# A batched-expert MLP on one core: the first four experts' input in other pieces, and one token order for all experts

## The chip, the cores and the metric

The kernel runs on 1 core of one Trainium2 chip. The metric is the device time of one execution in microseconds (us), as the median of several runs.

## What is computed

Eight experts, each with 256 tokens of 512 values, go through two layers with a ReLU between them:

```python
n_experts, capacity, hidden, expert_hidden = 8, 256, 512, 2048
...
h = np.matmul(x, w1)
h = np.maximum(h, 0)
return np.matmul(h, w2).astype(np.float32)
```

All arrays are float32. x and the output have 4.19 MB each, w1 and w2 33.6 MB each.

## The kernel before, in words

**Data.** The kernel computes in bf16. GpSimd (POOL) issues the weight loads as DMAs that cast float32 to bf16 on the way; both w1 and w2 have buffers for two experts (w1_sb, w2_sb). A load for expert e+2 waits until the first layer of expert e (for w1, semaphore s_first) or its second layer (for w2, s_act) is done. w2 of the last expert comes in two halves (s_w2 and s_w2b). x of experts 4 to 7 is also a casting DMA of POOL, into x_c. x of experts 0 to 3 comes in float32 on SP's queue into x_f, in three transfers (lines 107 to 109): expert 0 with 4 KB per partition, experts 1 and 2 together with 8 KB, expert 3 with 4 KB, each with a semaphore of its own.

**Transposing x.** Four rounds, two experts each. In a round DVE casts the even expert and ACT the odd one into x_b (line 200), PE transposes both through PSUM (L305), and DVE and ACT copy the result into xe (L216 or L225). xe holds x with the hidden index on the partitions and the tokens along the free axis. PE does all four rounds before its first matmul of the layers.

**Token order.** For pairs of experts the outputs are stored with four consecutive rows of the pair per partition, so that one partition's run in DRAM is 8 KB long. The order of the tokens within xe and ht decides which output row ends on which partition. Before the change the copies into xe produce the order that the first three pairs want, with one form for experts 0 and 3 and another for the others (lines 215 to 228); the last pair, stored per expert, has its order changed in the ReLU (lines 243 to 245).

**Layers.** For each of four pairs: first layer of both experts (64 matmuls each, L321, the weights from w1_sb, 256 tokens of xe as moving operand), ReLU by DVE and ACT from PSUM into ht (lines 248, 250), then second layer of both (32 matmuls each, L341) and copies into o_sb (L260). The program of PE is a hardware loop; addresses that change come from registers (function ahead).

**Who lets PE go on.** SP counts tokens for PE: it waits for a weight transfer's semaphore and then increments t_w, which PE takes before a first layer, before a second layer and, for the last expert, before its second half of w2 (kt = 8). SP also waits for s_xe, the copies into xe, ahead of the first experts' tokens.

**The end.** When the second layer of expert 6 is done (s_go), SP stores the first three pairs in one DMA of 3 MB (L137). Then it stores expert 6 in pieces: odd rows (64 partitions), every fourth row from 2 on (32 partitions), a token for PE in between, every fourth row in the middle (16 partitions) and the rest from a copy o_low (L149), and last expert 7 (512 KB) when its copies are done. In the code:

```python
sp.wait_ge(s_w2[e + b], 16).then_inc(t_w, 1)
store(E - 2, slice(1, P, 2))
store(E - 2, slice(2, P, 4))
sp.wait_ge(s_w2b, 16).then_inc(t_w, 1)
...
store(E - 2, slice(L, P - L, 4))
```

Of the kernel before, what the change touches and what calls it, by code (L numbers as in the profile page):

```python
# [9 lines left out]
def kernel(  # L10
# [7 lines left out]
    nc = tc.nc  # L18
# [26 lines left out]
    J = G * MT  # L45
    x_r = x.rearrange("e (p m) k -> p e m k", m=MT)
    x_pair = x[1:3].rearrange("e c k -> (e c) k").rearrange("(p s m) k -> p s m k", p=P, m=MT)
    x_rows = x[G:].rearrange("e c k -> (e c) k").rearrange("(p j) k -> p j k", p=P)


    x_f = nc.alloc_sbuf_tensor("x_f", [P, G, MT, H], f32)
    x_c = nc.alloc_sbuf_tensor("x_c", [P, J, H], bf)
    x_b = nc.alloc_sbuf_tensor("x_b", [P, 2, KT1 * MT, P], bf)
    xe = nc.alloc_sbuf_tensor("xe", [P, E * KT1 * C], bf)
# [18 lines left out]
    s_x = [sem(f"s_x{i}") for i in range(3)]  # L73
# [29 lines left out]
    def load_x(eng, e, n, src, i):  # L103
        ins = eng.dma_start(x_f[:, e:e + n], src).then_inc(s_x[i], 16)
        return ins.ins.name

    tc.no_tile_sem_insts.add(load_x(sp, 0, 1, x_r[:, :1], 0))
    tc.no_tile_sem_insts.add(load_x(sp, 1, 2, x_pair, 1))
    tc.no_tile_sem_insts.add(load_x(sp, G - 1, 1, x_r[:, G - 1:G], 2))
# [12 lines left out]
    for e in range(0, E, 2):  # L122
        for b in range(2):

            if e < G:
                sp.wait_ge(s_xe[b], e // 2 + 1)
                if e + b == 1:
                    sp.wait_ge(s_xe[0], 2)
            elif e + b == G:
                for s in s_xe:  # L130
                    sp.wait_ge(s, G)
            sp.wait_ge(s_w1[e + b if e else 0], 16).then_inc(t_w, 1)
        for b in range(2):
# [8 lines left out]
            else:  # L142
                sp.wait_ge(s_w2[e + b], 16).then_inc(t_w, 1)
                store(E - 2, slice(1, P, 2))
                store(E - 2, slice(2, P, 4))
                sp.wait_ge(s_w2b, 16).then_inc(t_w, 1)
    store(E - 2, slice(L, P - L, 4))
# [21 lines left out]
    pool.dma_start(x_c[:], x_rows).then_inc(s_xc, 16)  # L169
# [25 lines left out]
    def cast(eng, r, b):  # L195

        a = 2 * r + b
        src = x_f[:, a] if a < G else x_c[:, MT * (a - G):MT * (a - G + 1)]
# [6 lines left out]
    def take_x(eng, b):  # L205
        copy = act.copy if eng is act else dve.tensor_copy
        for r in range(G):
            if r < G // 2:
                eng.wait_ge(s_x[(2 * r + b + 1) // 2], 16)
            elif r == G // 2:  # L210
                eng.wait_ge(s_xc, 16)
            cast(eng, r, b)
            eng.wait_ge(s_tr, 2 * r + b + 1)
            a, n = 2 * r + b, KT1 * C
            if a in (0, G - 1):
                copy(  # L216
# [71 lines left out]

    def ahead(flat, weights, first, places, n, step=1):
        by = flat[:].bitcast(mybir.dt.uint8)
        aps = []
        for k in places:
# [87 lines left out]
```

## Time and profile before

| | |
|---|---|
| median of 3 runs | 178.99 us (178.84 to 178.99) |
| profiled execution: time, span | 178.96 us, 177.6 us |
| mean granted TensorE clock | 0.979 of full speed |
| busy: PE, DVE, ACT, POOL | 130.6 (74%), 39.5 (22%), 40.0 (23%), 10.3 (6%) us |
| DMA: POOL's casting queue, SP's queue | 34.60 MB and 91.6%, 6.29 MB and 8.7% of 16 engines' span |
| HBM read, written | 71.30 MB, 4.19 MB |
| chain that ended last | PE L341 2%, ACT L260 0.3% of the span |

The profile shows one execution. The span runs from the first to the last instruction; the time is 1.36 us longer. Bytes of a DMA are counted as they are written, so a cast from float32 to bf16 counts half of what it reads. DMA share is the mean busy share of 16 engines; over short stretches it can pass 1, since a packet counts where it starts.

### The profile page before, as it was taken

What the parts mean: (1) busy time and instruction counts of PE and PEld (TensorE: products, weight loads), DVE (VectorE), ACT (ScalarE), POOL (GpSimd) and SP (SyncE); (2) the same over time, 40 slices, a digit from 0 to 9 for tenths busy, and PEclk for the clock granted to TensorE, in tenths of its full rate; (3) what the DMA queues carried; (4) which work ended last, traced back from release to release, by engine and by line L of the source; (5) the groups of instructions that cost most, each with busy time, mean ns of one, the idle gap of its engine ahead of it and who ended that gap; (6) DMA issues with size and microseconds to landing.
All of it is one profiled execution on the core that took longest, in us unless ns stands there. A gap on an engine that the chain in (4) does not pass through costs nothing. (4 is left out here: it accounts for less than half of the span.)

```text
span 177.6 us, 2364 instructions
## 1 busy us (share of the span) xinstructions
PE 130.6 (74%) x832; PEld 88.9 (50%) x832; DVE 39.5 (22%) x54; ACT 40.0 (23%) x56; POOL 10.3 (6%) x22
## 2 busy tenths in 40 slices
PE   0034430598979699999969595979499695999890
PEld 0024420487854248788424485954134594874340
DVE  0142420123310306333030331320300431230101
ACT  2464520022220203323020222220200321220301
POOL 2400000001010101011010101010100200000000
PEclk9999999999999999999999999999969998799999
DMA  6999999999999999999999999999999999999998
GB/s 232 330 234 207 236 207 207 236 207 207 236 207 207 236 207 207 236 207 207 236 207 207 236 210 203 236 207 207 236 210 203 236 210 203 236 194 212 290 428 352
DMA packets 3720, 40.90 MB, mean 230 GB/s; under 512 B 392, under 2 KB 392, under 8 KB 904
## 3 DMA queue, kind: packets, MB, share of 16 engines
q0 software_dynamic: 2560, 34.60, 91.6%
q1 hardware_dynamic: 1160, 6.29, 8.7%
HBM read 71.30 MB, written 4.19 MB: 425 GB/s over the span
## 5 line engine op out<-in xcount | busy, mean ns | idle before, releaser
L321 PE MATMUL pt_h<-xe,w_sb 128*128 x512 | 65.3, 284 | 17.8 <-PEq L99 17.8
L321 PEld LDWEIGHTS pt_h<-xe,w_sb 128*128 x512 | 57.5, 147 | 26.2 <-issue 24.3
L341 PE MATMUL pt_o<-w_sb,ht_sb 128*128 x256 | 58.3, 386 | 8.7 <-PEq L99 8.7
L341 PEld LDWEIGHTS pt_o<-w_sb,ht_sb 128*128 x256 | 24.8, 99 | 40.9 <-issue 13.7
L250 DVE TENSOR_SCALAR ht_sb<-pt_h 128x512 bf16<-128x512 f32 x32 | 22.1, 692 | 56.1 <-PE pt_h L321 56.1
L248 ACT ACTIVATE ht_sb<-pt_h 128x512 bf16<-128x512 f32 x32 | 19.1, 597 | 61.4 <-PE pt_h L321 61.4
L260 DVE COPY out_sb<-pt_o 64x512 f32 (+1 forms) x14 | 9.6, 689 | 61.9 <-PE pt_o L341 61.8
L260 ACT COPY out_sb<-pt_o 64x512 f32 (+1 forms) x14 | 8.1, 582 | 59.3 <-PE pt_o L341 59.2
L305 PE MATMUL pt_tr<-identity,x_b 128*128 128x128 bf16 x64 | 7.5, 310 | 16.3 <-PEq L99 16.3
L305 PEld LDWEIGHTS pt_tr<-identity,x_b 128*128 128x128 bf16 x64 | 6.5, 144 | 17.0 <-issue 17.0
L159 POOL DMA_DIRECT2D w_sb<-in_w_dram x6 | 3.2, 534 | 74.6 <-ACTq L252 74.6
L225 DVE COPY xe<-pt_tr 128x1024 bf16<-128x1024 bf16 x3 | 3.3, 1088 | 7.9 <-PE pt_tr L305 7.9
L164 POOL DMA_DIRECT2D w_sb<-in_w_dram x5 | 2.6, 528 | 41.2 <-ACT out_sb L260 41.2
L225 ACT COPY xe<-pt_tr 128x1024 bf16<-128x1024 bf16 x3 | 3.6, 1196 | 6.1 <-PE pt_tr L305 6.1
L200 ACT CAST x_b<-x_f 128x1024 bf16<-128x1024 f32 x2 | 4.0, 1988 | 2.2 <-DMA x_f<-in_x_dram 2.2
L200 DVE CAST x_b<-x_f 128x1024 bf16<-128x1024 f32 x2 | 2.1, 1064 | 4.1 <-DMA x_f<-in_x_dram 4.1
L216 DVE COPY xe<-pt_tr 128x1024 bf16<-128x1024 bf16 x1 | 1.2, 1225 | 4.5 <-PE pt_tr L305 4.5
L200 ACT COPY x_b<-x_c 128x1024 bf16<-128x1024 bf16 x2 | 2.2, 1084 | 0.0
L156 POOL DMA_DIRECT2D w_sb<-in_w_dram x2 | 2.0, 1006 | 0.1
L200 ACT ACT_TABLE_LOAD x1 | 1.3, 1283 | 2.9 <-PEq L111 2.9
L216 ACT COPY xe<-pt_tr 128x1024 bf16<-128x1024 bf16 x1 | 1.0, 1012 | 2.0 <-PE pt_tr L305 2.0
L200 DVE COPY x_b<-x_c 128x1024 bf16<-128x1024 bf16 x2 | 1.4, 676 | 0.0
(10 smaller groups left out, 3.7 us busy)
## 6 DMA issues: line engine op xcount, KB each, us to landing
w_sb<-in_w_dram POOLq DMA_DIRECT2D x11, 2048.0 KB, 25.8
w_sb<-in_w_dram POOLq DMA_DIRECT2D x2, 4096.0 KB, 36.7
out_dram<-out_sb SPq DMA_DIRECT2D x1, 3072.0 KB
w_sb<-in_w_dram POOLq DMA_DIRECT2D x2, 1024.0 KB, 25.7
x_f<-in_x_dram SPq DMA_DIRECT2D x2, 512.0 KB, 4.7
x_f<-in_x_dram SPq DMA_DIRECT2D x1, 1024.0 KB, 5.3
x_c<-in_x_dram POOLq DMA_DIRECT2D x1, 1024.0 KB, 9.3
out_dram<-out_sb SPq DMA_DIRECT2D x1, 512.0 KB
```

The costliest lines, as they stand in the source:

```text
L156: pool.dma_start(dst.rearrange("p (e k) n -> p e k n", e=2), src).then_inc(s[0], 16)
L159: pool.dma_start(w1_k[:, e % 2 * KT1:(e % 2 + 1) * KT1], w1_r[e]).then_inc(s_w1[e], 16)
L164: pool.dma_start(w2_k[:, k:k + KT2], w2_r[e]).then_inc(s_w2[e], 16)
L200: copy(x_b[:, b].rearrange("p (t m) q -> p t m q", m=MT), src.rearrange("p m (q t) -> p t m q", t=KT1),).then_inc(t_xb, 1)
L216: copy(xe[:, a * n:(a + 1) * n].rearrange("p (j f r) -> p j f r", f=2, r=R), pt[b][:].rearrange("p j (r f) -> p j f r", f=2),).then_inc(s_ ...
L225: copy(xl[:, :, :, f, :, i].rearrange("p l j q -> p j l q"), pt[b][:].rearrange("p j (l q) -> p j l q", l=l),).then_inc(s_xe[b], 1)
L248: act.activation(dst, src, relu).then_inc(t_h, 1)
L250: dve.tensor_relu(dst, src).then_inc(t_h, 1)
L260: ins = copy(dst, src)
L305: ins = pe.transpose(pt[b][:, j], x_b[:, b, j], identity[:])
L321: ins = pe.matmul(ph[i // 2][:, i % 2, :], ws[i % 2 * KT1 + kt], xs[kt], start=(kt == 0), stop=(kt == KT1 - 1),)
L341: ins = pe.matmul(po[:, m], hs[(kt - k0) * MT + m], ws[kt - k0], start=(kt == 0), stop=(kt == KT2 - 1),)
```

## The change

x of expert 0 comes in two transfers of 2 KB per partition (one row of x each), and x of experts 1 to 3 in one transfer of 12 KB per partition. The first has semaphore s_x0, which now reaches 32, the second s_x1. A partition holds six consecutive rows of the three experts' 768, so that each of the three casts and transposes touches tokens of all three experts, and the copies into xe write every third element (every fourth for experts 4 to 7, which had a step of two). xe is laid out by hidden block and row half, with all 1024 token pairs side by side in natural order, so the moving operand of a first-layer matmul is two runs of 128 columns instead of one of 256. The change of order for the first three pairs is now made in their ReLU, and the last pair's ReLU reads in order. SP waits ahead of expert 1's token for the copies of experts 0 to 3. The store of 32 partitions of expert 6 follows the wait for s_w2b instead of standing ahead of it.

```diff
@@ -42,16 +42,17 @@
-    J = G * MT
-    x_r = x.rearrange("e (p m) k -> p e m k", m=MT)
-    x_pair = x[1:3].rearrange("e c k -> (e c) k").rearrange("(p s m) k -> p s m k", p=P, m=MT)
-    x_rows = x[G:].rearrange("e c k -> (e c) k").rearrange("(p j) k -> p j k", p=P)
-
-
-    x_f = nc.alloc_sbuf_tensor("x_f", [P, G, MT, H], f32)
-    x_c = nc.alloc_sbuf_tensor("x_c", [P, J, H], bf)
+    W = E * P
+    PARTS = ((0, 1), (1, G), (G, E))
+
+    def x_rows(e0, e1):
+        return x[e0:e1].rearrange("e c k -> (e c) k").rearrange("(p j) k -> p j k", p=P)
+
+    x_f = nc.alloc_sbuf_tensor("x_f", [P, MT * G, H], f32)
+    x_c = nc.alloc_sbuf_tensor("x_c", [P, MT * (E - G), H], bf)
     x_b = nc.alloc_sbuf_tensor("x_b", [P, 2, KT1 * MT, P], bf)
-    xe = nc.alloc_sbuf_tensor("xe", [P, E * KT1 * C], bf)
+    xe = nc.alloc_sbuf_tensor("xe", [P, KT1 * MT * W + W - P], bf)
+    xe_j = xe[:, :KT1 * MT * W].rearrange("p (j t) -> p j t", t=W)
     w1_sb = nc.alloc_sbuf_tensor("w1_sb", [P, 2 * KT1 * F + KT2], bf)
     w2_sb = nc.alloc_sbuf_tensor("w2_sb", [P, 2 * KT2 * H], bf)
     ht = nc.alloc_sbuf_tensor("ht_sb", [P, 2 * KT2, H], bf)
@@ -70,7 +71,7 @@
     pt = [nc.alloc_psum_tensor(f"pt_tr{b}", [P, KT1 * MT, P], bf) for b in range(2)]
     sem = nc.alloc_semaphore
-    s_x = [sem(f"s_x{i}") for i in range(3)]
+    s_x = [sem(f"s_x{i}") for i in range(2)]
     s_xc = sem("s_xc")
     s_out = sem("s_out")
     s_go = sem("s_go")
@@ -100,13 +101,11 @@
-    def load_x(eng, e, n, src, i):
-        ins = eng.dma_start(x_f[:, e:e + n], src).then_inc(s_x[i], 16)
-        return ins.ins.name
-
-    tc.no_tile_sem_insts.add(load_x(sp, 0, 1, x_r[:, :1], 0))
-    tc.no_tile_sem_insts.add(load_x(sp, 1, 2, x_pair, 1))
-    tc.no_tile_sem_insts.add(load_x(sp, G - 1, 1, x_r[:, G - 1:G], 2))
+    for s, (e0, e1) in zip(s_x, PARTS):
+        step = 1 if e0 == 0 else MT * (e1 - e0)
+        for j in range(0, MT * (e1 - e0), step):
+            ins = sp.dma_start(x_f[:, MT * e0 + j:MT * e0 + j + step], x_rows(e0, e1)[:, j:j + step])
+            tc.no_tile_sem_insts.add(ins.then_inc(s, 16).ins.name)
     tc.close()
     tc.compile()
@@ -122,13 +121,10 @@
     for e in range(0, E, 2):
         for b in range(2):
-            if e < G:
-                sp.wait_ge(s_xe[b], e // 2 + 1)
-                if e + b == 1:
-                    sp.wait_ge(s_xe[0], 2)
-            elif e + b == G:
-                for s in s_xe:
-                    sp.wait_ge(s, G)
+            for e0, e1 in PARTS:
+                if e + b == e0:
+                    for i in range(2 if e0 else 1):
+                        sp.wait_ge(s_xe[i], (e1 + 1 - i) // 2)
             sp.wait_ge(s_w1[e + b if e else 0], 16).then_inc(t_w, 1)
         for b in range(2):
             if e + b == E - 1:
@@ -142,8 +138,8 @@
             else:
                 sp.wait_ge(s_w2[e + b], 16).then_inc(t_w, 1)
                 store(E - 2, slice(1, P, 2))
-                store(E - 2, slice(2, P, 4))
                 sp.wait_ge(s_w2b, 16).then_inc(t_w, 1)
+    store(E - 2, slice(2, P, 4))
     store(E - 2, slice(L, P - L, 4))
     sp.wait_ge(s_low, 1)
     sp.dma_start(out_q[::4, ::3], o_two).then_inc(s_out, 16)
@@ -166,7 +162,7 @@
             pool.dma_start(w2_k[:, k:k + CUT], w2_r[e, :, :CUT]).then_inc(s_w2[e], 16)
             pool.dma_start(w2_k[:, k + CUT:k + KT2], w2_r[e, :, CUT:]).then_inc(s_w2b, 16)
-    pool.dma_start(x_c[:], x_rows).then_inc(s_xc, 16)
+    pool.dma_start(x_c[:], x_rows(G, E)).then_inc(s_xc, 16)
     load_pair(w1_k, w1, s_w1)
     pool.memset(identity[:], 0.0).then_inc(s_id, 1)
     pool.wait_ge(s_id, 1)
@@ -195,7 +191,7 @@
     def cast(eng, r, b):
         a = 2 * r + b
-        src = x_f[:, a] if a < G else x_c[:, MT * (a - G):MT * (a - G + 1)]
+        src = x_f[:, MT * a:MT * (a + 1)] if a < G else x_c[:, MT * (a - G):MT * (a - G + 1)]
         copy = act.copy if eng is act else dve.tensor_copy
         copy(
             x_b[:, b].rearrange("p (t m) q -> p t m q", m=MT),
@@ -205,27 +201,17 @@
     def take_x(eng, b):
         copy = act.copy if eng is act else dve.tensor_copy
         for r in range(G):
-            if r < G // 2:
-                eng.wait_ge(s_x[(2 * r + b + 1) // 2], 16)
-            elif r == G // 2:
-                eng.wait_ge(s_xc, 16)
+            a = 2 * r + b
+            for s, (e0, e1) in zip((*s_x, s_xc), PARTS):
+                if e0 <= a < min(e0 + 2, e1):
+                    eng.wait_ge(s, 16 if a else 16 * MT)
             cast(eng, r, b)
             eng.wait_ge(s_tr, 2 * r + b + 1)
-            a, n = 2 * r + b, KT1 * C
-            if a in (0, G - 1):
-                copy(
-                    xe[:, a * n:(a + 1) * n].rearrange("p (j f r) -> p j f r", f=2, r=R),
-                    pt[b][:].rearrange("p j (r f) -> p j f r", f=2),
-                ).then_inc(s_xe[b], 1)
-            else:
-                e0, l = (1, 2) if a < G else (G, G)
-                f, i = (a - e0) % 2, (a - e0) // 2
-                xl = xe[:, e0 * n:(e0 + l) * n].rearrange(
-                    "p (l j f q i) -> p l j f q i", l=l, j=KT1 * MT, f=2, i=l // 2)
-                copy(
-                    xl[:, :, :, f, :, i].rearrange("p l j q -> p j l q"),
-                    pt[b][:].rearrange("p j (l q) -> p j l q", l=l),
-                ).then_inc(s_xe[b], 1)
+            e0, e1 = next(part for part in PARTS if part[0] <= a < part[1])
+            copy(
+                xe_j[:, :, e0 * P:e1 * P].rearrange("p j (q i) -> p j q i", i=e1 - e0)[:, :, :, a - e0],
+                pt[b][:],
+            ).then_inc(s_xe[b], 1)
@@ -240,9 +226,9 @@
                     k = KT2 * b + FB * q + FB // 2 * half
                     dst, i = ht[:, k:k + FB // 2, :C], NQ * b + q + 1
                     src = ph[half][:]
-                    if last:
-                        dst = dst.rearrange("p k (m r f) -> p k m r f", m=MT, f=2)
-                        src = src.rearrange("p k (m f r) -> p k m r f", m=MT, f=2)
+                    if not last:
+                        dst = dst.rearrange("p k (m f r) -> p k m f r", m=MT, f=2)
+                        src = src.rearrange("p k (m r f) -> p k m f r", m=MT, f=2)
                     eng.wait_ge(s_h, i)
                     if eng is act:
                         act.activation(dst, src, relu).then_inc(t_h, 1)
@@ -288,11 +274,13 @@
-    def ahead(flat, weights, first, places, n, step=1):
+    def ahead(flat, weights, first, places, n, step=1, rows=1):
         by = flat[:].bitcast(mybir.dt.uint8)
         aps = []
         for k in places:
             ap = by[:, bass.ds(first + 2 * k, 2 * n * step)].bitcast(bf)
+            if rows > 1:
+                ap = ap.rearrange("p (m n) -> p m n", m=rows)[:, :, :P]
             aps.append(ap if step == 1 else ap.rearrange("p (n s) -> p n s", s=step)[:, :, 0])
             pe.lower_ap(aps[-1], for_matmul_weights=weights)
         return aps
@@ -307,7 +295,7 @@
     with pe.Fori(0, G) as g:
         with pe.Fori(0, 2) as b:
-            xs = ahead(xe, False, g * (4 * KT1 * C) + b * (2 * KT1 * C), [kt * C for kt in range(KT1)], C)
+            xs = ahead(xe, False, g * (4 * P) + b * (2 * P), [kt * MT * W for kt in range(KT1)], MT * W, rows=MT)
             take(t_w)
             with pe.Fori(0, NQ) as q:
                 for i in range(FB):
```

The instructions of SP, before. These are its DMAs in program order, with the semaphores waited for ahead of each; x_f is x in float32, out_sb the output on chip:

```order
L104 DMA x_f<-in_x_dram 128x1024
L104 DMA x_f<-in_x_dram 128x2048
L104 DMA x_f<-in_x_dram 128x1024
...
L137 DMA out_dram<-out_sb 128x3x2048 [waits barrier_Pool_Activation_PE_DVE_SP_release,s_w1_0,s_xe0,s_xe1,s_w2_0,s_dve,s_act,s_w1_2,s_w1_3,s_w2_2,s_w2_3,s_w1_4,s_w1_5,s_w2_4,s_w2_5,s_w1_6,s_w1_7,s_w2_6,s_go]
L120 DMA out_dram<-out_sb 64x1024 [waits s_dve,s_w2_7,s_act]
L120 DMA out_dram<-out_sb 32x1024
L120 DMA out_dram<-out_sb 16x1024 [waits s_w2b]
L149 DMA out_dram<-out_sb 8x2x1024 [waits s_low]
L120 DMA out_dram<-out_sb 128x1024 [waits s_dve,s_act]
```

And of the changed kernel:

```order
L107 DMA x_f<-in_x_dram 128x512 x2
L107 DMA x_f<-in_x_dram 128x3072
...
L133 DMA out_dram<-out_sb 128x3x2048 [waits barrier_Pool_Activation_PE_DVE_SP_release,s_w1_0,s_xe0,s_xe1,s_w2_0,s_dve,s_act,s_w1_2,s_w1_3,s_w2_2,s_w2_3,s_w1_4,s_w1_5,s_w2_4,s_w2_5,s_w1_6,s_w1_7,s_w2_6,s_go]
L119 DMA out_dram<-out_sb 64x1024 [waits s_dve,s_w2_7,s_act]
L119 DMA out_dram<-out_sb 32x1024 [waits s_w2b]
L119 DMA out_dram<-out_sb 16x1024
L145 DMA out_dram<-out_sb 8x2x1024 [waits s_low]
L119 DMA out_dram<-out_sb 128x1024 [waits s_dve,s_act]
```

The x transfers are 2 + 1 instead of 1 + 1 + 1, and the wait for s_w2b has moved ahead of the store of 32 partitions.

ACT's part in the four rounds before (x_b is the cast input of the transposes, pt_tr their output):

```order
L200 CAST x_b<-x_f 128x1024 [waits s_x1]
L225 COPY xe<-pt_tr 128x8x2x64 [waits s_tr]
L200 CAST x_b<-x_f 128x1024 [waits s_x2]
L216 COPY xe<-pt_tr 128x1024 [waits s_tr]
L200 COPY x_b<-x_c 128x1024 [waits s_xc]
L225 COPY xe<-pt_tr 128x8x4x32 [waits s_tr]
```

And in the changed kernel:

```order
L196 CAST x_b<-x_f 128x1024 [waits s_x1]
L211 COPY xe<-pt_tr 128x8x128 [waits s_tr]
L196 CAST x_b<-x_f 128x1024
L211 COPY xe<-pt_tr 128x8x128 [waits s_tr]
L196 COPY x_b<-x_c 128x1024 [waits s_xc]
L211 COPY xe<-pt_tr 128x8x128 [waits s_tr]
```

The casts are as many as before; s_x1 now stands for experts 1 to 3, and all copies into xe have one form.

## Rows read from the trace of the kernel before

**Rows 1.** The page's 40 slices of the span: busy tenths of the DMA engines.

```profile
DMA  6999999999999999999999999999999999999998
```

**Rows 2.** Stretches in us: each engine's busy time, granted clock, DMA share, GB/s.

```profile
1.00:1.60 0.60, 0.00 (x0) 0.00 (x0) 0.00 (x0) 0.00 (x0) 0.00 (x0) 1.00 0.00 0
1.60:2.40 0.80, 0.00 (x0) 0.00 (x0) 0.00 (x0) 0.00 (x0) 0.00 (x0) 1.00 0.79 179
2.40:3.00 0.60, 0.00 (x0) 0.00 (x0) 0.00 (x0) 0.05 (x1) 0.00 (x0) 1.00 0.94 375
3.00:7.00 4.00, 0.00 (x0) 0.00 (x0) 1.07 (x1) 1.76 (x2) 3.16 (x5) 1.00 1.01 419
7.00:167.00 160.00, 124.24 (x804) 86.30 (x805) 37.72 (x52) 37.53 (x54) 6.90 (x13) 0.98 1.02 217
167.00:167.25 0.25, 0.25 (x3) 0.12 (x2) 0.00 (x0) 0.06 (x1) 0.00 (x0) 1.00 0.53 197
167.25:174.25 7.00, 6.13 (x28) 2.45 (x26) 0.69 (x1) 0.58 (x1) 0.00 (x0) 1.00 1.02 431
174.25:177.00 2.75, 0.00 (x0) 0.00 (x0) 0.00 (x0) 0.00 (x0) 0.00 (x0) 0.97 0.99 399
```

**Rows 3.** Timeline: start, duration, engine, line, operation, [idle before <- what ended it].

```profile
6.47 1.99 ACT L200 CAST x_b<-x_f 128x1024 bf16<-128x1024 f32 x1 [2.24 <-DMA x_f<-in_x_dram]
...
23.79 1.28 ACT L225 COPY xe<-pt_tr 128x1024 bf16<-128x1024 bf16 x1 [2.05 <-PE pt_tr L305]
...
32.91 1.48 PE L321 MATMUL pt_h<-xe,w_sb 128*128 x6 [9.16 <-PEq L99]
```

**Rows 4.** Timeline of SP at the end, its issues of stores.

```profile
166.07 2.16 SPq L120 DMA_DIRECT2D out_dram<-out_sb  x1
168.28 1.37 SPq L120 DMA_DIRECT2D out_dram<-out_sb  x1
174.11 0.35 SPq L120 DMA_DIRECT2D out_dram<-out_sb  x1
```

**Rows 5.** Timeline of PE in the second layer of expert 7.

```profile
166.15 7.31 PE L341 MATMUL pt_o<-w_sb,ht_sb 128*128 x32 [0.88 <-PEq L99]
...
169.39 0.38 PE L341 MATMUL pt_o<-w_sb,ht_sb 128*128 x1
...
169.85 0.38 PE L341 MATMUL pt_o<-w_sb,ht_sb 128*128 x1
```

**Rows 6.** The page's count of DMA packets.

```profile
DMA packets 3720, 40.90 MB, mean 230 GB/s; under 512 B 392, under 2 KB 392, under 8 KB 904
```

**Rows 7.** The tile x_f: SP's issues (ns min/median/max, first and last start), and landing.

```profile
L104 SPq DMA_DIRECT2D x_f<-in_x_dram x3: 391/412/432, 0.7 to 1.6; - x3
...
DMA to landing us min/median/max: 3.3/5.3/6.1
```

**Rows 8.** The tile xe: copies at line 225, ns min/median/max.

```profile
L225 ACT COPY xe<-pt_tr x3: 1012/1281/1296, 10.5 to 23.8; 128x1024 bf16<-128x1024 bf16 x3
L225 DVE COPY xe<-pt_tr x3: 692/1284/1287, 14.6 to 22.9; 128x1024 bf16<-128x1024 bf16 x3
```

**Rows 9.** The tile ht_sb: the ReLUs, ns min/median/max.

```profile
L250 DVE TENSOR_SCALAR ht_sb<-pt_h x32: 690/692/693, 34.9 to 157.5; 128x512 bf16<-128x512 f32 x32
L248 ACT ACTIVATE ht_sb<-pt_h x32: 597/597/597, 36.6 to 158.4; 128x512 bf16<-128x512 f32 x32
```

**Rows 10.** The page's costliest groups: weight loads, busy us, mean ns, idle before.

```profile
L321 PEld LDWEIGHTS pt_h<-xe,w_sb 128*128 x512 | 57.5, 147 | 26.2 <-issue 24.3
...
L341 PEld LDWEIGHTS pt_o<-w_sb,ht_sb 128*128 x256 | 24.8, 99 | 40.9 <-issue 13.7
```

**Rows 11.** Timeline of PE's second-layer passes, and a stretch with its granted clock.

```profile
119.46 7.07 PE L341 MATMUL pt_o<-w_sb,ht_sb 128*128 x32 [1.32 <-PEq L99]
129.11 8.70 PE L341 MATMUL pt_o<-w_sb,ht_sb 128*128 x32 [2.58 <-PEq L99]
...
130.00:132.00 2.00, 2.00 (x6) 0.66 (x5) 0.00 (x0) 0.00 (x0) 0.00 (x0) 0.50 0.96 205
```

## The prediction

> **What bounds the kernel now.** Begin with the page's 40 slices. The DMA row stands at 9 from the second slice to the last but one [rows 1], so the question is which part of the 16 DMA engines' work could be shorter. The table of stretches answers it [rows 2]. No byte moves until 1.60 us. From 1.60 to 2.40 the engines move 179 GB/s, then 375, and from 3.00 to 7.00 they are full at 419. From 7.00 to 167.00 the DMA share is 1.02; these are the cast loads, whose rate is counted as written in bf16 and so reads about half of what HBM gives. From 167.25 on the stores run at 431 and then 399 GB/s, up to 177.0. It is one transfer after another with no hole above 0.12 us (0.25 us at a share of 0.53). The span is therefore the start, the DMA work, and 0.6 us for the last receipt. An edit counts if it changes the start-up, the amount of DMA work, or the moment at which the last store can join the queue.
>
> Then see what is covered. The first layer begins at 32.91 us, after PE had waited 9.16 for its weights' token, and the last copy into xe begins at 23.79 and takes 1.28 [rows 3]: the x work has 7.8 us to spare. Later weight loads lie back to back (the share of 1.02), so PE, DVE and ACT have room in the middle as well. At the end two chains run side by side: the queue of stores, and PE's last 32 matmuls with the copies and SP's last store, issued at 174.11 [rows 4, 5].
>
> **The change, part by part.**
>
> *Amount of DMA work in x.* Before: 128 rows of 4 KB, 128 of 8 KB, 128 of 4 KB. After: 128 and 128 of 2 KB, 128 of 12 KB. Both are 384 rows, 24 for each engine, and 2.1 MB. The page counts rows one by one: 904 packets under 8 KB less 392 small ones are 512, the 256 rows of x and 256 of the stores that have 4 KB [rows 6]. What a row costs beside its bytes is read from the stores, whose 8 KB rows go first and 4 KB rows last: 8192 x 16 / 431 = 304 ns, and 4096 x 16 / 399 = 164 ns, so two small rows take 24 ns more than one large. As many rows before and after: 0. Were a 12 KB row cut in two, it would be 8 more rows per engine, 8 x 24 = 0.19 us; no row of the trace shows 12 KB, and I take 0 because 8 KB ones are not cut.
>
> *Start-up.* The first transfer now has 2 KB rows. Up to 3.00 us the engines move 0.8 x 179 + 0.6 x 375 = 368 KB, where 419 GB/s would be 587 KB: 219 KB, or 0.52 us, are lost there now [rows 2]. No row shows 2 KB loads into idle engines, so both ends: if small rows fill the engines at once, 0.52 us comes back; if each row in that stretch takes as long as a 4 KB row does now, only half the 368 KB move and 184 KB / 419 = 0.44 us is lost. I take 0, between the two: SP's three issues take about 0.41 us each from 0.7 on [rows 7], so two of them bring 512 KB by about 1.6 us, while the engines have used 143 KB by 2.40. They are not short of issued work before or after.
>
> *One boundary more ahead of expert 1.* The three transfers land 3.3 to 6.1 us after their issues at 0.7 to 1.6, that is at about 4.1, 6.47 (where ACT's cast begins) and 7.7 us [rows 3, 7]. The middle one is 1.05 MB in 2.4 us, some 440 GB/s: between transfers of one queue nothing is lost, and there are three before and after. Cost 0.
> The Trainium skill, page "DMA: Bandwidth & Descriptors", section "Anatomy of one DMA — SWDGE (gpsimd) path", fits 2.0 us plus bytes / 436 GB/s for each DMA on GpSimd's path, and its section "Rules for kernel authors" asks for at least 1 MiB per DMA, which speaks against 256 KB pieces of x of expert 0. If each of SP's pieces paid that alone, the sum would be 2.0 us worse; the landings above disagree with it.
>
> *Cover of x.* Expert 1's cast now waits for all of experts 1 to 3, the same bytes that land by 7.7 us now: ACT starts 1.2 us later, and each round of transposes behind it. The copies into xe write with a step of 3 or 4 elements for seven experts. Stepped ones (2 elements) take 1.28 to 1.30 us, even ones at least 0.69 on DVE and 1.01 on ACT [rows 8], so ACT has 0.3 us more in each of two rounds: 1.2 + 0.6 = 1.8 us later at the end, under the 7.8 to spare. SP's longer wait at expert 1 stands ahead of a token that PE can't use before its w1 lands; behind it on SP are other tokens and no DMA until 165. Cost 0, as long as the last copy ends before 32.9 us.
>
> *Relu in another order.* Now the first three pairs read PSUM with a step and the last pair reads evenly; before it was the last pair that had the other order, and all 32 relus of each engine, those eight included, take 690 to 693 ns on DVE and 597 on ACT [rows 9]. Cost 0.
>
> *First-layer matmuls* read their 256 columns as two runs of 128. No row has that. Bounds are 0 and, from the weight loads, whose stepped form takes 147 ns against 99 [rows 10], 48 ns in each of 64 matmuls, 3.1 us an expert. That step is at every element, ours is one break in 256, so I take 0.
>
> *The store moved behind the wait for w2b.* SP issues the store of 64 rows at 166.07 for 2.16 us, that of 32 rows at 168.28 for 1.37, to 169.65, and only then comes to the wait that frees PE for the second half of expert 7 [rows 4]. PE starts a matmul at 169.39 and the next at 169.85, where its pace is 7.31 / 32 = 0.23 us [rows 5]: 0.23 us lost to SP. After the change the token comes at about 168.3 and the last store is issued 0.23 us earlier; the 32-row store and the ones behind it keep their places. Is that worth anything? The six earlier stores are 3.67 MB. By 174.25 some 3.05 MB have gone [rows 2]; 0.62 MB at 399 GB/s last until 175.8, while a store issued at 174.11 can start by 175.0 (first byte 0.9 us after the issue, as 0.7 to 1.6 shows). It stands in line for 0.8 us, so an earlier issue buys nothing. Against that, x's first 0.5 MB took 3.3 us from issue to landing with nothing ahead of it, and the last store takes no more than 177.6 - 174.1 = 3.5. Bounds 0 and -0.23; I take -0.1.
>
> **Sum.** 0 for x, 0 for compute, -0.1 at the end. The profiled execution took 178.96 us (its span and 1.36 around it) against a median of 178.99, so they are used alike: **178.9 us**, with 178.65 to 179.2 for this case alone. About 0.2% (0.36 us) is what a measurement of this kernel can tell from no change.
>
> **Rivals.**
> 1. *Forecast*, a change within 0.2%: 0.58.
> 2. *Small first rows fill the engines sooner.* For it: the share from 1.60 to 2.40 is only 0.79. Half of the 0.52 comes back, and at the end 0.23: 178.99 - 0.26 - 0.23 = 178.5. Against it: the engines idle there with rows already issued. 0.20, faster.
> 3. *Small first rows starve them.* Place: the first 1.4 us of transfers; price +0.44, to 179.4; it decides if a row there takes a fixed time whatever its size. For it: 179 GB/s at a share of 0.79 means that a 4 KB row holds its engine for about 290 ns, against 156 at 419 GB/s. Against it: only two or three rows per engine fall in that stretch. 0.15, slower.
> 4. *PE's last pass falls to the low clock.* From 130 to 132 us the granted clock was 0.50 (1.2 GHz of 1.2 and 2.4) after PE had idled 2.58, and that pass of 32 matmuls took 8.70 instead of 7.07 us [rows 11]. In the last pass, after its 0.88 us of idling [rows 5], the last store would come 1.63 - 0.23 = 1.4 us later, of which the queue hides 0.8: 179.6. It decides above 0.8 us. Against it: only the shorter idling. 0.05, slower.
> 5. *Each transfer pays a fixed price alone.* x's first took 3.3 us, less 1.25 for its bytes leaves 2.05 for one small transfer more ahead of expert 1, if it delays the whole queue: 181.0. Against it: the landings. 0.02, slower. This is what the fit of the Trainium skill's page named above would make of it.
>
> **How the numbers follow.** Faster 0.20 (case 2), within 0.2% 0.58, slower 0.22 (cases 3, 4, 5). The range 178.4 to 179.45 holds cases 1 to 3 and the price of a cut row; cases 4, 5 and the far ends of 2 and 3 stay outside.
>
> **What would show it.** In the changed profile: the x loads end and the cast loads begin at about 7.0 us; the stretch 1.6 to 3.0 moves 368 KB, clearly more for case 2, some 184 for case 3; ACT's first cast begins near 7.7 and the last copy into xe ends before 28; the gap ahead of the second half of expert 7 on PE is gone and the last store is issued some 0.23 us earlier; the DMA row is full until the stores end. I am wrong if the cast loads end at another time than the x loads' end explains, or if the span shrinks by as much as the last store moves.

## The result and the profile after

The change makes the kernel slower: 181.48 us median (181.39 to 181.73) against 178.99 (178.84 to 179.13) on the same chip, 1.0139 times the time before (1.0125 to 1.0153). The forecast was 178.9, with 178.4 to 179.45 as its range. The profiled execution of the changed kernel took 181.49 us, 2.53 more than that of before.

The start comes first, since [rows 2] had the engines full from 3.00 us. The table of stretches of the changed kernel (columns as in [rows 2]):

```profile
1.60:2.40 0.80, 0.00 (x0) 0.00 (x0) 0.00 (x0) 0.00 (x0) 0.00 (x0) 1.00 0.63 220
2.40:3.00 0.60, 0.00 (x0) 0.00 (x0) 0.00 (x0) 0.05 (x1) 0.00 (x0) 1.00 0.97 352
3.00:7.00 4.00, 0.00 (x0) 0.00 (x0) 1.07 (x1) 1.23 (x1) 3.27 (x5) 1.00 0.94 314
3.20:4.60 1.40, 0.00 (x0) 0.00 (x0) 0.00 (x0) 1.03 (x1) 1.24 (x2) 1.00 0.66 199
4.60:7.00 2.40, 0.00 (x0) 0.00 (x0) 1.07 (x1) 0.00 (x0) 2.03 (x4) 1.00 1.03 369
7.00:167.00 160.00, 121.31 (x791) 85.89 (x799) 39.81 (x51) 40.20 (x52) 7.10 (x14) 0.99 1.02 218
...
169.75:176.75 7.00, 5.75 (x26) 2.45 (x25) 0.69 (x1) 0.59 (x1) 0.00 (x0) 1.00 1.00 415
176.75:180.00 3.25, 0.00 (x0) 0.00 (x0) 0.00 (x0) 0.00 (x0) 0.00 (x0) 1.00 0.67 267
```

Until 3.00 us the new kernel moves 0.8 x 220 + 0.6 x 352 = 387 KB, 19 KB more than before. Then comes a hole: from 3.00 to 7.00 it moves 314 GB/s instead of 419, and most of that lies in 3.20 to 4.60, at 199 GB/s, where the kernel before has this row:

```profile
3.20:4.60 1.40, 0.00 (x0) 0.00 (x0) 0.52 (x1) 1.03 (x1) 1.24 (x2) 1.00 1.05 439
```

So 105 x 4.00 = 420 KB were not moved by 7.00, 1.0 us at 419 GB/s. The cast loads then run at the old pace (a share of 1.02 and 218 GB/s), but the end comes 2.5 us later, so a mean over the engines explains less than half.

The rest shows in the semaphore increments. The trace shows 16 increments of a transfer's semaphore, as many as there are DMA engines. They are read here as one from each engine when its part of the transfer is done; the trace does not name the engine. Whoever waits for 16 goes on with the last. These are the trace's times of the increments of the first pair of w1, which lets PE begin (us, sorted):

```
before         31.62 31.63 31.64 31.71 31.73 31.75 31.76 31.77 31.84 31.98 31.99 32.00 32.07 32.08 32.10 32.14
after          32.32 32.38 32.40 32.43 32.54 32.65 32.66 32.67 32.69 32.72 32.93 33.07 33.67 34.17 34.19 34.45
halves_before  32.60 32.67 32.69 32.74 32.81 32.82 32.86 33.20 34.04 34.12 34.15 34.17 34.32 34.34 34.47 34.51
whole_x0       31.64 31.65 31.67 31.74 31.77 31.79 31.80 31.84 31.85 31.88 31.90 31.93 31.95 32.01 32.03 32.06
```

Before, they lie within 0.52 us; after, within 2.13. The middle of them is 0.88 us later (31.80 to 32.68), the last 2.31 (32.14 to 34.45). The spread was there when x of experts 1 to 3 landed (8.18 to 11.49 us; before, x of expert 3: 7.44 to 7.71), and is still there 136 us later (second half of w2 of expert 7: 167.91 to 170.08, before 167.27 to 167.73). So an engine that falls behind stays behind, and the kernel goes at the pace of the last one; that it is the same engines throughout is inferred from a spread that keeps its size. PE's and ACT's timelines of the changed kernel, against [rows 3]:

```profile
11.51 1.98 ACT L196 CAST x_b<-x_f 128x1024 bf16<-128x1024 f32 x1 [7.28 <-DMA x_f<-in_x_dram]
...
31.40 2.42 ACT L211 COPY xe<-pt_tr 128x1024 bf16<-128x1024 bf16 x1 [2.05 <-PE pt_tr L293]
...
35.22 9.96 PE L309 MATMUL pt_h<-xe,w_sb 128*128 x63 [3.86 <-PEq L100]
```

PE begins at 35.22, 0.77 us after the last increment (34.45); before it was 32.91 - 32.14 = 0.77 too. So w1 lets it go and not the last copy into xe, though that now ends at 33.82 instead of 25.07. The copies, against [rows 8]:

```profile
L211 DVE COPY xe<-pt_tr x4: 692/2142/2425, 14.7 to 30.5; 128x1024 bf16<-128x1024 bf16 x4
L211 ACT COPY xe<-pt_tr x4: 1870/2148/2433, 15.5 to 31.4; 128x1024 bf16<-128x1024 bf16 x4
```

The end, SP's stores against [rows 4] and PE against [rows 5]:

```profile
168.40 5.06 SPq L119 DMA_DIRECT2D out_dram<-out_sb  x3
173.51 1.41 SPq L145 DMA_DIRECT2D out_dram<-out_sb  x1
176.20 0.34 SPq L119 DMA_DIRECT2D out_dram<-out_sb  x1
...
168.49 7.07 PE L329 MATMUL pt_o<-w_sb,ht_sb 128*128 x31 [0.88 <-PEq L100]
```

PE's pass is 7.07 us instead of 7.31, and the last store comes 2.09 us later than before (174.11), where PE's pass began 2.34 later: the 0.24 that PE's pass is shorter reached the last store. But the span ends 4.0 us after it instead of 3.5. The stores meet engines that are up to 2 us apart, and the last stretch is at a share of 0.67 (0.99 before).

### The profile page after: what moved, and what is told of

The parts are those of the page before. It is cut to its first block, busy times and chain, and to the rows that moved or that the text cites. A ratio compares the mean times of both kernels' runs of the same rounds, so it can differ in the third digit from the quotient of the medians.

```text
span 180.2 us, 2356 instructions
## 1 busy us (share of the span) xinstructions
PE 128.9 (72%) x824; PEld 89.0 (49%) x832; DVE 42.3 (23%) x54; ACT 43.7 (24%) x56; POOL 10.6 (6%) x22
## 2 busy tenths in 40 slices
DMA packets 3720, 40.90 MB, mean 227 GB/s; under 512 B 392, under 2 KB 392, under 8 KB 904
## 5 line engine op out<-in xcount | busy, mean ns | idle before, releaser
L329 PE MATMUL pt_o<-w_sb,ht_sb 128*128 x248 | 56.1, 379 | 9.8 <-PEq L100 9.4
L211 DVE COPY xe<-pt_tr 128x1024 bf16<-128x1024 bf16 x4 | 7.4, 1850 | 17.9 <-PE pt_tr L293 17.9
L211 ACT COPY xe<-pt_tr 128x1024 bf16<-128x1024 bf16 x4 | 8.6, 2150 | 8.2 <-PE pt_tr L293 8.2
L167 POOL MEMSET identity<- 128x128 bf16 x1 | 1.1, 1102 | 0.0
```

Source lines behind the costliest of these rows:

```text
L167: pool.memset(identity[:], 0.0).then_inc(s_id, 1)
L211: copy(xe_j[:, :, e0 * P:e1 * P].rearrange("p j (q i) -> p j q i", i=e1 - e0)[:, :, :, a - e0], pt[b][:],).then_inc(s_xe[b], 1)
L329: ins = pe.matmul(po[:, m], hs[(kt - k0) * MT + m], ws[kt - k0], start=(kt == 0), stop=(kt == KT2 - 1),)
```

## The experiments

The letters are those of the expectations. A: rows of 12 KB stall. B: the 2 KB rows of expert 0's two short transfers do. C: the slower copies into xe. D: a limited rate of rows. E: a price for each transfer. F: SP's queue hands its transfers over one behind the other, and one of 256 KB is too short to cover the handing over of the next. G: F does not hold, and the number of transfers or GpSimd's later start decides. H: the halves, each of which reads every second 2 KB, disturb what is beside or behind them. P and S, for the stalled rows: GpSimd's transfers take part, or SP's queue alone. The kernel before, run beside each, had medians of 178.99 to 179.17.

**Which part of the change.** cut_12k cuts the long transfer, whole_x0 joins the two short ones; both stand in the changed kernel:

```diff
+    CUTS = {0: ((0, 1), (1, 2)), 1: ((0, 4), (4, 6))}   # cut_12k
+    CUTS = {0: ((0, 2),), 1: ((0, 6),)}                 # whole_x0
+        for j, k in CUTS[e0]:
+            ins = sp.dma_start(x_f[:, MT * e0 + j:MT * e0 + k], x_rows(e0, e1)[:, j:k])
```

> The changed kernel with the 12 KB rows of experts 1 to 3 cut in two transfers, 8 KB and 4 KB a partition; x of expert 0 stays in 2 KB halves, the token order and the copies stay. Theory A (the 12 KB rows are what stalls the DMA engines between 3.2 and 4.6 us of the changed kernel): the stretch 3.2 to 4.6 is full again (share 1.0), the first matmul of the first layer is back near 33 us, time about 178.9 (178.6 to 179.2). Theory B (the 2 KB rows of expert 0 drain before the next rows are there, so that the engines run dry at 3.2 us): the stretch stays near 0.66, first matmul near 35.2, time about 181.4. Theory C (slower copies into xe and their waits, not the DMA): also about 181.4, but with a full stretch.

> The changed kernel with x of expert 0 in one transfer of 4 KB rows, and the 12 KB rows of experts 1 to 3 kept. Theory A (12 KB rows): still slow, about 181.4, the stretch after the first transfer at a share well under 1. Theory B (2 KB rows): the stall is gone, about 178.9, first matmul near 33 us. Theory C (copies): about 181.4 with a full stretch.

The other two start from the kernel before, with one part of the change each:

```diff
-    tc.no_tile_sem_insts.add(load_x(sp, 0, 1, x_r[:, :1], 0))      # halves_before
+    for m in range(MT):
+        ins = sp.dma_start(x_f[:, 0, m:m + 1], x_r[:, 0, m:m + 1]).then_inc(s_x[0], 16)

-                store(E - 2, slice(2, P, 4))                       # store_moved
                 sp.wait_ge(s_w2b, 16).then_inc(t_w, 1)
+    store(E - 2, slice(2, P, 4))
```

> The kernel before, with nothing changed but x of expert 0 in two transfers of 2 KB rows, so four transfers of x in all. Theory A (12 KB rows): no change, 178.8 to 179.2, first matmul at 32.9. Theory B (2 KB rows): about 181.4, first matmul near 35.2. Theory C (copies): no change.

> The kernel before, with nothing changed but the store of 32 partitions of expert 6 behind the wait for the second half of w2. Prediction's step: PE's gap at 169.4 to 169.85 goes, the last store is issued 0.23 us earlier, and since the stores stand in line the time falls by 0 to 0.23 us, about 0.1: 178.9. If the queue of stores sets the end alone: 179.0. If the last store's own way sets it: 178.75.

Measured: cut_12k 181.70 us, 1.0133 (1.0107 to 1.0160); whole_x0 179.03, 0.9994 (0.9983 to 1.0004); halves_before 181.66, 1.0144 (1.0122 to 1.0167); store_moved 179.06, 1.0000 (0.9988 to 1.0013). A falls, since whole_x0 keeps the 12 KB rows and cut_12k has none; C falls, since whole_x0 keeps the new copies. The two halves alone, put into the kernel before, cost the whole difference. The hole of cut_12k, which has no 12 KB rows:

```profile
3.20:4.60 1.40, 0.00 (x0) 0.00 (x0) 0.23 (x1) 1.18 (x1) 0.76 (x2) 1.00 0.42 132
```

Stretches of whole_x0:

```profile
3.00:7.00 4.00, 0.00 (x0) 0.00 (x0) 1.06 (x1) 0.75 (x1) 3.34 (x5) 1.00 1.06 430
3.20:4.60 1.40, 0.00 (x0) 0.00 (x0) 0.47 (x1) 0.55 (x1) 1.40 (x3) 1.00 1.19 483
```

and of halves_before:

```profile
3.00:7.00 4.00, 0.00 (x0) 0.00 (x0) 1.06 (x1) 1.28 (x1) 2.79 (x5) 1.00 0.79 251
3.20:4.60 1.40, 0.00 (x0) 0.00 (x0) 0.29 (x1) 1.18 (x1) 0.76 (x2) 1.00 0.51 173
```

The same hole, in the same place, is there with halves and gone without. In store_moved SP's last store was issued 0.19 us earlier (174.11 before), near the 0.23 of the prediction, and the time stayed the same to within its interval, about 0.2 us on either side:

```profile
173.92 0.34 SPq L120 DMA_DIRECT2D out_dram<-out_sb  x1
```

**Small rows, or short transfers?** half_parts makes the halves of 64 partitions with 4 KB rows; rows_2k_once is one transfer for expert 0, but of 2 KB rows (a gap of one row in x_f keeps them apart); x0_last puts the 12 KB transfer first; rows_16k is one transfer for experts 0 to 3, whose cast has to wait for all of it.

```diff
+        ins = sp.dma_start(x_f[R * h:R * (h + 1), :MT], x_rows(0, 1)[R * h:R * (h + 1)])  # half_parts
+    ins = sp.dma_start(x_f[:, :MT + 1:MT], x_rows(0, 1))                                  # rows_2k_once
+    for s, (e0, e1) in reversed(tuple(zip(s_x, PARTS))):                                  # x0_last
+    ins = sp.dma_start(x_f[:], x_rows(0, G))                                              # rows_16k
```

> The changed kernel, with x of expert 0 in two transfers of 64 partitions each, rows of 4 KB, instead of two of 128 partitions with rows of 2 KB: the same number of transfers and bytes, half the rows. Theory D (SP's queue brings rows at a limited rate, some 150 per us, whatever their size; 2 KB rows are used up as fast as they come, so the engines run dry when x of expert 0 is through): no stall, first matmul at 32.9, about 179.0. Theory E (each transfer ahead of the large one costs a time of its own, some 0.9 us): the stall stays, first matmul near 35, about 181.4.

> The changed kernel, with x of expert 0 in one transfer again, but with a gap between its two rows on chip, so that each partition still receives two rows of 2 KB: half the transfers, the same 256 rows. Theory D (rate of rows): the stall stays, share well under 1 from 3.2 to 4.6 us, about 181.4. Theory E (price per transfer): no stall, about 179.0.

> The changed kernel with the order of SP's loads turned round: the 12 KB rows of experts 1 to 3 first, the two transfers of 2 KB rows of expert 0 behind them. Theory D: the 12 KB rows last longer than it takes to bring the 256 small ones, so no engine runs dry; x of expert 0 lands at about 7.5 us instead of 4.6, which the 7.8 us to spare hide: about 179.0. Theory E: the small transfers no longer stand ahead of the large one and their time is hidden by its 3.6 us: about 179.0 too. If 2 KB rows are slow by themselves wherever they stand: 179.5 to 181.4.

> The changed kernel with x of experts 0 to 3 in one transfer of 16 KB rows, 128 rows in all. Theory D: rows come far faster than they are used, and the start fills sooner than with 4 KB rows: the loss of 0.52 us before 3.0 us shrinks to some 0.2 to 0.4, time 178.7 to 179.0. If the slow start is the latency of the first bytes and not the rate of rows: no change from 179.0. Expert 0's cast waits for all four experts (some 7.5 us), hidden by the time to spare.

half_parts 180.77 us, 1.0113 (1.0066 to 1.0159); rows_2k_once 179.56, 1.0020 (1.0004 to 1.0035); x0_last 179.51, 1.0025 (1.0011 to 1.0039); rows_16k 179.65, 1.0027 (1.0015 to 1.0039). rows_2k_once has all the 2 KB rows and no hole, so D falls, and it is not the rows:

```profile
3.20:4.60 1.40, 0.00 (x0) 0.00 (x0) 0.00 (x0) 1.04 (x1) 1.22 (x2) 1.00 1.18 468
```

Its 0.5 us is the late start: SP takes 728 ns for that issue instead of about 400, and the first row starts at 2.25 us. rows_16k saves two transfers and gains nothing: E falls as the main price, and so does D's forecast of 178.7 to 179.0 for that run. x0_last has both short transfers at the end of the queue, where GpSimd's work is behind them. half_parts is inconclusive: its issues took 572 to 608 ns, and its 4 KB rows from 3.3 us on 235 to 318 ns instead of 159.

**Behind whom?** act_queue leaves the halves on SP's queue and issues the 12 KB transfer from ACT; four_512k has four transfers of 512 KB; half_12k_half puts the long transfer between the halves.

```diff
+            eng = act if e0 else sp                                        # act_queue
+    CUTS = {0: ((0, 2),), 1: ((0, 2), (2, 4), (4, 6))}                     # four_512k
+        (s_x[0], x_f[:, :1], x_0[:, :1]),                                  # half_12k_half
+        (s_x[1], x_f[:, MT:], x_rows(1, G)),
+        (s_x[0], x_f[:, 1:MT], x_0[:, 1:]),
```

> The changed kernel with the 12 KB transfer of experts 1 to 3 issued by ACT on its own queue at the start, instead of third on SP's; the two 2 KB transfers of expert 0 stay on SP. Theory F (SP's queue hands its transfers to the engines one after the other, some 0.9 us each whatever the row size; 256 KB last only 0.61 us at 419 GB/s, so the third transfer's rows come late): the 12 KB rows no longer stand behind the halves, the engines have work from the start, no stall at 3.2 to 4.6 us, first matmul at 33 to 33.4, time 178.9 to 179.4. Rival H (the halves themselves, each reading every second 2 KB, disturb what runs beside or behind them, whatever queue it is on): stall and 181 or more.

> The changed kernel with x of expert 0 in one transfer and x of experts 1 to 3 in three of 4 KB rows: four transfers of 512 KB, one more than in the slow kernel. Theory F: each lasts 1.25 us, longer than the 0.9 us in which the next is handed over, so the engines stay full: first matmul at 32.9, 178.9 to 179.2, though POOL starts 0.46 us later (3.84). Rival G (every transfer more on SP costs, by itself or by POOL's later start): slower than the changed kernel or like it, 181 to 182.

> The changed kernel with SP's order 2 KB half, 12 KB transfer, 2 KB half: only one short transfer stands ahead of the large one. Theory F: the engines run short once, by 0.9 - 0.61 = 0.3 us, not twice: between the two, 179.2 to 180.3. Rival G (number of transfers): like the changed kernel, 181.4. Rival H (halves disturb what is behind them): like the changed kernel or somewhat better.

act_queue 179.68 us, 1.0035 (1.0021 to 1.0050), 0.3 above what F forecast at most, and the hole is gone:

```profile
3.20:4.60 1.40, 0.00 (x0) 0.00 (x0) 0.00 (x0) 0.56 (x1) 1.28 (x3) 1.00 1.04 418
```

These are the same three transfers with the same rows, so H falls, and so does "three transfers are too many". The long transfer's rows now start at 2.08 us, and expert 0's second half lands only at 14.86. What hurts in the change is a long transfer queued behind two short ones. half_12k_half has one short one ahead: 180.15 median, but from 179.45 to 180.68 in single runs, 1.0065 (1.0045 to 1.0084). four_512k goes against F: 180.52 median, yet 179.30 in the profiled run and 180.42 to 180.68 in the four others; that is not explained by short transfers, since it has none.

**The rows that stall.** In the changed kernel a 12 KB row normally takes 460 ns. Of the first sixteen, which start between 3.15 and 4.43 us (3.45 and 3.76 in whole_x0), five take over 1.1 us; four more that start at 4.70 to 4.92 take 1.16 to 1.78 us. GpSimd issues its first transfers from 3.36 us on, so three runs move them: pool_late holds it until x of experts 1 to 3 has landed, and the x_c_early pair issues x_c ahead of the barrier, in the changed kernel and in the one before. four_512k_again is the same kernel as four_512k, for another profile.

```diff
+    pool.wait_ge(s_x[1], 16)                                               # pool_late
     pool.dma_start(x_c[:], x_rows(G, E)).then_inc(s_xc, 16)

+    tc.no_tile_sem_insts.add(pool.dma_start(x_c[:], x_rows(G, E)).then_inc(s_xc, 16).ins.name)  # x_c_early
     tc.close()
```

> The changed kernel, in which GpSimd issues its first transfer (x of experts 4 to 7) only when x of experts 1 to 3 has landed. Theory P, GpSimd's transfers take part in the second stall: no row of x takes over 1 us after 4.6 us, x of experts 1 to 3 lands before 9 us (11.7 us was the landing of GpSimd's x in the change), the increments of the first w1 pair on the 16 engines spread by under 1 us (2.1 in the change), though the whole comes later by the time that the engines idle. Theory S, the stall belongs to SP's queue alone: rows of over 1 us after 4.6 us and the spread of about 2 us stay, and the time is well over 181.5 us.

> The same kernel as four_512k (x of experts 0 to 3 in four transfers of 512 KB), to have a profile of its slower mode. Theory F with a stall as in the change: where the time is about 180.5 us, the profile has x rows of over 1 us and a spread of the first w1 pair's increments of over 1.2 us; where it is about 179.3, neither. If the slower mode shows no long rows and no spread, the modes have another cause and stay open.

> The changed kernel, with GpSimd's first transfer (x of experts 4 to 7) issued before the barrier, at about the time of SP's first. Theory F, the loss is DMA time in which no rows are there: GpSimd's rows fill the holes, the stretch 3.20 to 4.60 us has a share over 0.95, and the time is 179.0 to 179.8 us. Theory P, GpSimd's transfers make the stall: long rows stay or come earlier, and the time is 181 us or more.

> The kernel before, with the same earlier issue by GpSimd. Theory F: the rows of both queues stand ready from the first microsecond; the stretch 1.60 to 3.00 us moves more than the 368 KB of before, and the time is 178.99 less up to 0.5 us. If the start is limited by something else, 178.8 to 179.2 us; if the two queues hinder each other, over 179.4 us.

pool_late 184.64 us, 1.0295 (1.0255 to 1.0335): GpSimd's first issue is at 10.22 us, yet ten rows take over 1 us (one of them starts after 4.6), and x lands over 7.71 to 9.92. P falls by the trace of the changed kernel itself: GpSimd's first packet starts at 7.51 us, and the last of the slow rows had ended at 6.70. S's forecast of a lasting spread did not come either: w1's increments in pool_late lie within 0.71 us, though x's lie 2.21 apart. GpSimd began there only when every engine was done with x, so nothing was queued that could have kept the skew; that is an argument, no run tests it. four_512k_again 180.47, 1.0066 (1.0043 to 1.0089): behind the first sixteen, rows of x of up to 0.49 us instead of 0.16 (0.40 in the profile that took 179.30), none longer, and a w1 spread of 1.20 us (0.71 there). Its last increment comes at 33.66 instead of 32.53 and explains the time. What its trace does show are slow rows on the other queue: seven of GpSimd's first rows, which start at 7.52 to 7.85, take 1.36 to 1.89 us, where 0.62 is usual and none takes over 1 us in the other profile. Why they are slow stays open. The early x_c told something else than it was meant to, 185.04 us, 1.0314 (1.0284 to 1.0344), and 182.82, 1.0198 (1.0174 to 1.0221). GpSimd issues w1 late:

```profile
13.46 0.91 POOL L157 DMA_DIRECT2D w_sb<-in_w_dram  x1 [11.59 <-POOLq L112]
```

That is x_c_early_before, where GpSimd's drain ahead of the barrier lasts from 1.20 to 12.45 us and x_c's increments come at 12.43 to 12.79: the barrier opened only then, so the engines ran dry ahead of w1. The times therefore try neither theory. The rows of x_c_early_after do: with GpSimd's rows there from 3.27 us on, the stretch 3.20 to 4.60 has a share of 1.06 and no 12 KB row takes over 0.70 us, which is F's sign and not P's. But four of GpSimd's first rows now take 1.03 to 2.21 us.

The last two hold the long transfer back until both halves have landed. In x_after_halves the wait came to stand behind SP's third issue instead of ahead of it; x_after_halves_2 has the issue behind the barrier and the wait.

```diff
+        if e0:                                                             # x_after_halves
+            sp.wait_ge(s_x[0], 16 * MT)

+    sp.wait_ge(s_x[0], 16 * MT)                                            # x_after_halves_2
+    sp.dma_start(x_f[:, MT:MT * G], x_rows(1, G)).then_inc(s_x[1], 16)
```

> The changed kernel, in which SP issues the transfer of experts 1 to 3 only when both halves of expert 0 have landed, at about 4.3 us. If the stalls need the short transfers still under way on the same queue: no row of 12 KB takes over 1 us, the 16 increments of that transfer come within 1 us of each other at about 9 to 9.5 us, and the time is 180.3 to 181.2 us, since the engines idle for about a microsecond between 4.3 and 5.3 us. If the stalls come with any 12 KB transfer behind two short ones: rows of over 1 us and a spread of about 2 us remain and the time is over 182 us.

> The changed kernel, with SP's transfer of experts 1 to 3 taken out of the first block and issued behind the barrier, after a wait for both halves of expert 0 (x_after_halves had only moved the wait behind the issue). If the stalls need the short transfers still under way on the same queue: no row of 12 KB takes over 1 us before GpSimd's rows start, the 16 increments of that transfer come within 1.2 us of each other at about 9 to 10 us, and the time is 180.0 to 181.3 us, the engines idling for about a microsecond. If a 12 KB transfer that comes third stalls anyway: rows of over 1 us and a spread of about 2 us or more, and over 182 us.

x_after_halves 181.71 us, 1.0142 (1.0123 to 1.0161). The wait delayed only the other engines, GpSimd's first issue to 5.42, and three rows that started at 4.82 to 4.96 took 1.83 to 1.95 us: a second sign against P. x_after_halves_2 181.00, 1.0107 (1.0090 to 1.0123), with no 12 KB row over 0.47 us, though they start only at 7.85, among GpSimd's, and land at 18.61 to 20.39 instead of the 9 to 10 that was expected. That fits stalls that need the short transfers still under way, but the same trace speaks against it: eleven of GpSimd's first thirteen rows, which come to the emptied engines at 4.24 to 4.52, take 1.03 to 1.81 us. So slow rows are not tied to SP's queue, to rows of 12 KB or to short transfers still under way.

**One number for every run.** If the last of the 16 increments of w1's first pair sets the pace, the profiled time must be 178.96 + (last increment - 32.14):

| run | last increment | worked out | profiled time |
|---|---|---|---|
| after | 34.45 | 181.27 | 181.49 |
| whole_x0 | 32.06 | 178.88 | 179.13 |
| halves_before | 34.51 | 181.33 | 181.54 |
| rows_2k_once | 32.63 | 179.45 | 179.57 |
| x0_last | 32.62 | 179.44 | 179.89 |
| act_queue | 32.98 | 179.80 | 179.68 |
| four_512k, four_512k_again | 32.53, 33.66 | 179.35, 180.48 | 179.30, 180.46 |
| pool_late | 37.65 | 184.47 | 184.46 |
| x_c_early_after | 38.41 | 185.23 | 185.20 |
| x_after_halves_2 | 33.98 | 180.80 | 180.90 |

The runs not shown differ by at most 0.25; the largest difference is x0_last's 0.45. The middle increment would not do: it gives 179.84 for the changed kernel and 180.92 for x_after_halves, which took 181.49 and 182.08. The rule of the last one holds even in x_after_halves_2, where x came so late that PE began its layers at 40.07 us instead of 32.91:

```profile
40.07 9.46 PE L311 MATMUL pt_h<-xe,w_sb 128*128 x64
```

So a PE that begins 7 us late costs nothing that the table leaves to explain, and an engine that is 2 us late costs 2. No variant beat the kernel before; whole_x0 equals it.

## Why the prediction was wrong

- **The bound was right.** The DMA work sets the span: the shift of w1's last increment gives every profiled time to within 0.45 us, even where PE began 7 us late.
- *Amount of DMA work in x*: right. The page again counts 3720 packets and 904 under 8 KB, so 12 KB rows are not cut, and the usual row takes 84, 159, 309 and 460 ns for 2, 4, 8 and 12 KB, near the estimate of 304 and 164 ns for 8 and 4. The slow rows were not foreseen.
- *Start-up*: right up to 3.00 us (387 KB against 368; cases 2 and 3 both fell), wrong behind it. "They are not short of issued work before or after" counted bytes that SP had issued. The two halves are 524 KB, of which 387 had moved by 3.00; at 419 GB/s the other 137 KB last until 3.3 us, and 231 of the 256 rows had started by then, the last one at 4.17. The third transfer, issued by 2.08, had only seven of its 128 rows started by 3.67 and its sixteenth at 4.43: issued is not the same as ready for an engine.
- *One boundary more ahead of expert 1* is the step that failed. "Between transfers of one queue nothing is lost" came from the landings of 512 KB and 1 MB transfers, and was carried over to 256 KB ones, which no row showed. halves_before adds that boundary, with the 2 KB rows that go with it, and costs 2.58 us (181.66 against 179.08 beside it), the whole effect; the change without the boundary (whole_x0) has 179.03 us, and the same rows without it (rows_2k_once) cost 0.5. The step took one value where it needed a bound on either side for a transfer that no row showed.
- Rival 5 had the sign and, at 181.0, nearly the size, at a chance of 0.02. Its mechanism, a price of 2.05 us for one small transfer more, is not what the runs show: in act_queue the same pieces cost 0.6, and rows_16k with one transfer gains nothing. What was near was its number. The Trainium skill's page that stood with it, "DMA: Bandwidth & Descriptors", section "Rules for kernel authors", asks for at least 1 MiB per DMA; here 256 KB pieces did cost and 512 KB ones, in the kernel before, did not (four of them, in four_512k, cost 1.5 in most runs), so the rule had the right side and the landings of larger pieces were no case against it.
- *Cover of x*: the cost was 0 as predicted, but the cover was nearly used up. "ACT has 0.3 us more in each of two rounds" was mis-sized: a step of 3 takes 1.87 us and one of 4 takes 2.43, on both engines, where a step of 2 took 1.28. ACT's four copies have 8.6 us instead of 4.6. The last copy ended at 33.82, not before 28; 5.0 us of the 8.75 are the late landing, the rest the copies.
- *Relu in another order* and *First-layer matmuls*: right. ReLUs take 691 to 693 and 597 to 598 ns, and matmuls a median of 273 ns before and after.
- *The store moved*: the 0.23 at PE and SP came nearly whole, in the change (0.25) and in store_moved (0.19, 173.92 against 174.11). What it is worth in time can't be told: store_moved's interval, about 0.2 us on either side of 0, holds both the -0.1 and the 0 that the store's wait in line would give. The earlier stores are five, not six; their 3.67 MB are right.

What stays open: why a transfer behind two short ones on its queue is fed late and unevenly (F names it, no record shows it); why a second group of slow rows starts at 4.6 to 5.1 us in the changed kernel, cut_12k, halves_before and x_after_halves alike; and why four_512k has two times.

## What to carry to other kernels

Do not take a split at the start of a DMA-bound kernel as free because the issues keep up. Here they did: a 256 KB piece lasts 0.6 us at 419 GB/s and its issue takes 0.4, and what was queued behind two of them still came late. Run the split alone, and look at when the rows behind it start. Where transfers are spread over 16 engines without a pause, read the last increment and not the mean share: what one engine loses early is lost at the end. Price a strided copy by a row with that very stride.

## What the runs showed that was not expected

- A skew between the DMA engines of 2.1 us, made in the first 10 us, was still 2.17 us (167.91 to 170.08) at the end; 135 us of queued work did not level it.
- The first long rows on idle engines take longer: in x0_last the first sixteen 12 KB rows took 0.87 to 1.37 us against 460 ns, without a lasting skew (0.64 us in w1). The first six 2 KB rows of the changed kernel took 81 to 109 ns against 84.
- Copies from PSUM with single bf16 elements stepped in the output cost the same on DVE and ACT (step 3: 1.87 us, step 4: 2.43 us per 1024 elements), where even ones differ (0.69 and 1.01).
- A transfer that GpSimd issued ahead of the barrier held the barrier until it was landing (increments at 12.43 to 12.79 us, POOL's next issue at 13.46; in x_c_early_after 14.92 and 16.01).
